# A hybrid trunk in fp32: gate and branch projections turned token-major, with 512 streamed weight columns

## Chip, cores and metric

The kernel runs on 1 core of a Trainium2 chip. The metric is the device time of one launch in microseconds; 977.33 is the median of three runs of the kernel before.

## What is computed

Two layers of a residual block on 256 tokens x 1024 channels, all in fp32. The part that the change touches is the parallel branches and their gated sum:

```python
u = rms_norm(h, norm_mix_pre[l])
proj = u @ w_in[l]
q, k, v, xr, yr, pp, gt = jnp.split(proj, SPLITS, axis=-1)
attn_br = sliding_window_attention(q, k, v, attn_sinks[l]) @ w_attn_br[l]
xc = causal_depthwise_conv(xr, conv_w[l], conv_b[l])
hr = rg_lru(xc, ...)
rnn_br = (hr * jax.nn.gelu(yr)) @ w_rnn_br[l]
pool_br = multi_scale_pool(pp, w_pool_groups[l], pool_scale[l]) @ w_pool_br[l]
g = jax.nn.sigmoid(gt).reshape(b, s, N_BRANCHES, D_MODEL)
merged = g[:, :, 0] * attn_br + g[:, :, 1] * rnn_br + g[:, :, 2] * pool_br
mix = merged @ w_out[l]
h = h + rms_norm(mix, norm_mix_post[l])
m = rms_norm(h, norm_mlp_pre[l])
h = h + rms_norm(jnp.square(jax.nn.relu(m @ w_mlp_up[l])) @ w_mlp_down[l], norm_mlp_post[l])
```

Each of the three gates and of the three branch projections is a 1024 x 1024 matrix.

## The kernel before

**Numbers.** Every fp32 operand is split into a high part (rounded to the `fp32r` format that TensorE multiplies) and a low part, the rest. A product is three matmuls, high x high, high x low and low x high (`mm3`, lines 88 to 91; these three lines stand for nearly all matmuls of the profile). The split is one ScalarE copy and one VectorE subtraction (`split`, lines 79 to 86).

**Weights.** They come as a stream of 512 KB half units [128, 1024] in the order of use: a DMA to `raw` (4 buffers), the split into `wh` and `wl` (8 buffers each; lines 81 and 82), then use. `take(n)` hands over the next n half units, `ahead()` asks for the splits of the two after them (lines 127 to 157).

**Two forms of a product.** In `w_unit` (line 273) the weights stand still: each 128x128 block of them is loaded and the 256 tokens are streamed past, so a matmul has 256 columns and the result is feature-major [128 features, 256 tokens]. One unit takes two half units and makes 256 features in one PSUM bank, with 48 matmuls. In `s_hu` (line 286) the tokens stand still: a 128x128 block of the activations is loaded and 512 weight columns are streamed past it, so the result is token-major [128 tokens, 512 features]; a half unit takes 6 matmuls per token tile, 12 for both. The output projection and the MLP's `down` use `s_hu`; `up`, the gates and the branches use `w_unit`. q, k, v use the token-major form by passes (`by_pass`, line 296).

**Order of the branch part.** The string `ORDER` lists the units: pp, yr, xr are input projections of the pool and recurrent branches, pg the pool's group products, gp/ga/gr the gates and bp/ba/br the branch projections (p pool, a attention, r recurrent), each 1024-column matrix in four units of 256. Every unit ends with `tick()`, a counter; `later(d, f)` runs f d ticks on. In this way the attention's scores, transposes and value products (four groups, scores at ticks 2, 7, 12 and 17; groups 1 and 3 are the large ones, with 256 keys, 4 score banks and 4 banks `pT` of transposed probabilities) and the recurrent gates are mixed into the projections. The instruction order of each engine is then fixed by a list scheduler at build time; `residual`, `mix_norm` and the transposes of `mlp_in(0)` run at a higher priority.

**Gated sum.** `gate` (line 600) makes th = tanh(x/2) on ScalarE from the unit's bank (line 603). `project` (line 607) forms (th + 1) times the projection on VectorE (lines 613 and 615), adds it to `merged[j]` (line 616), and, after the last branch (r), splits half of `merged[j]` into `mh`, `ml` (lines 84 and 85, tiles mgh and mgl in the profile), which are feature-major already.

**Output projection** (lines 638 to 663): eight half units, i = 0 to 3 for the first 512 output columns, contraction chunks 0-1, 2-3, 4-5, 6-7, and 4 to 7 for the second 512 columns. Token tile 0 runs through all eight, then tile 1; the post-norm `residual(0)` works meanwhile, and the transposes of `mlp_in(0)` (line 213, reading the updated `h`) are mixed into tile 1.

All PSUM tiles come from one pool of 8 banks.

Of the kernel before, what the change touches and what calls it, by code (L numbers as in the profile page):

```python
# [12 lines left out]
AF = mybir.ActivationFunctionType  # L13
# [5 lines left out]
T = 256  # L19
# [15 lines left out]
FINE = (8, 8)  # L35
SQRT_2_PI = 0.7978845608028654

# order of the units between q, k, v and the output projection: pp/yr/xr projections, pg pool groups,
# g gates and b branch projections of the branches p (pool), a (attention), r (recurrent)
ORDER = (  # L40
    "pp0 gp0 pp1 gp1 pp2 gp2 pp3 gp3 yr0 yr1 pg0 pg1 yr2 yr3 bp0 bp1 bp2 bp3 "
    "xr0 ga0 xr1 ga1 xr2 ga2 xr3 ga3 ba0 ba1 ba2 ba3 gr0 gr1 br0 gr2 br1 gr3 br2 br3"
).split()

# columns of the parameter tile, per layer
PG_PRE, PG_MLP, PCONVW, PCONVB, PBA, PBI, PLAM, PSCALE, PSINK = 0, 8, 16, 48, 56, 64, 72, 80, 88
NPAR = 104

# [1 line left out]
def trunk(ctx, tc, x, wts, rgw, par, gpost, eye, ctab, out):  # L50
# [19 lines left out]
    def ttile(shape, dt=F32, nm="t"):  # L70
        return tmp.tile(shape, dt, tag="t", name=nm)
# [7 lines left out]
    def split(hi, lo, src, scale=None):  # L79
        if scale is None:  # L80
            A.activation(hi, src, AF.Copy)  # L81
            V.tensor_tensor(out=lo, in0=src, in1=hi.bitcast(F32), op=ALU.subtract)  # L82
        else:
            A.activation(hi, src, AF.Copy, scale=scale)
            V.scalar_tensor_tensor(out=lo, in0=src, scalar=scale, in1=hi.bitcast(F32),
                                   op0=ALU.mult, op1=ALU.subtract)
# [3 lines left out]
        PE.matmul(o, lh, rl, start=False, stop=False, **kw)  # L90
        PE.matmul(o, ll, rh, start=False, stop=stop, **kw)  # L91

# [1 line left out]
    h = const.tile([P, 2, D], F32, name="h")  # L94
    idt = const.tile([P, P], F32, name="idt")
    cst = const.tile([P, ctab.shape[1]], F32, name="cst")
# [19 lines left out]
    for i in range(WARM):  # L116
        PE.matmul(wps[:], warm[:, 0:P], warm[:], start=True, stop=True)

# [1 line left out]
    NHU = wts.shape[0]  # L120
    st = {"load": 0, "split": 0, "use": 0}
    raw_t, hu_t = {}, {}
# [27 lines left out]
    def take(n):  # L150
        split_to(st["use"] + n)
        r = [hu_t.pop(st["use"] + i) for i in range(n)]
        st["use"] += n
        return r
# [10 lines left out]
    def tick():  # L165
        clock["n"] += 1
        run = [f for n, f in due if n <= clock["n"]]
        due[:] = [(n, f) for n, f in due if n > clock["n"]]
        for f in run:
            f()  # L170
# [2 lines left out]
        while due:  # L173
            tick()

# [1 line left out]
    hb = const.tile([P, L, 16], F32, name="hb")  # L177
    kk = const.tile([P, L, 8], F32, name="kk")
    nk2 = const.tile([P, L, 8], F32, name="nk2")
# [24 lines left out]
        V.tensor_scalar(kk[:], q, 2.0, None, op0=ALU.mult)  # L204
        V.tensor_scalar(nk2[:], q, -4.0, None, op0=ALU.mult)

# [1 line left out]
    def to_features(tt, src, gain, hi, lo, between=None):  # L208
        """src (token-major halves) * gain -> feature-major high and low parts."""
        tsl = slice(tt * P, (tt + 1) * P)  # L210
        banks = [bank([P, 4, P]) for _ in range(2)]
        for c in range(8):
            PE.transpose(banks[c // 4][:, c % 4, :], src[c // 4][:, (c % 4) * P:(c % 4 + 1) * P], ident)  # L213
        for half in range(2):
            if half and between:
                between()
            cs = range(4 * half, 4 * half + 4)
            for c in cs:
                A.activation(hi[:, c, tsl], banks[half][:, c % 4, :], AF.Copy, scale=gain[:, c:c + 1])  # L219
            for c in cs:  # L220
                V.scalar_tensor_tensor(out=lo[:, c, tsl], in0=banks[half][:, c % 4, :], scalar=gain[:, c:c + 1],
                                       in1=hi[:, c, tsl].bitcast(F32), op0=ALU.mult, op1=ALU.subtract)
# [25 lines left out]

    @hp
    def residual(tt, banks, scale, gB):  # L250
        """h[tt] += gB * scale * banks / rms(scale * banks)"""
        yg = []
        ss = stile(2)
        for nh in range(2):
            square_sum(banks[nh][:], ss[:, nh:nh + 1], scale)
            t = ttile([P, 512], nm="yg")
            gs = gB[:, nh * 512:(nh + 1) * 512]
            if isinstance(scale, float):
                V.tensor_tensor(out=t[:], in0=banks[nh][:], in1=gs, op=ALU.mult)
            else:  # L260
                V.scalar_tensor_tensor(out=t[:], in0=banks[nh][:], scalar=scale, in1=gs, op0=ALU.mult, op1=ALU.mult)
            yg.append(t)
        rs = rsqrt(total(ss))
        for nh in range(2):
            sl = slice(nh * 512, (nh + 1) * 512)
            V.scalar_tensor_tensor(out=h[:, tt, sl], in0=yg[nh][:], scalar=rs, in1=h[:, tt, sl],  # L266
                                   op0=ALU.mult, op1=ALU.add)
# [3 lines left out]
                acts.tile([P, NC_, T], F32R, tag="lo", name=nm + "l"))  # L271

    def w_unit(hus, xh, xl):
        """[128, 2, 256] = two column chunks of W (8 contraction chunks in 2 half units), times x."""
        ps = bank([P, 2, T])
        for n in range(2):
            for i, (wh, wl) in enumerate(hus):
                a = wh.rearrange("p (k n) -> p k n", k=4)
                b = wl.rearrange("p (k n) -> p k n", k=4)
                for k in range(4):  # L280
                    c = 4 * i + k
                    mm3(ps[:, n, :], a[:, k, n * P:(n + 1) * P], b[:, k, n * P:(n + 1) * P],
                        xh[:, c, :], xl[:, c, :], c == 0, c == 7)
        return ps
# [8 lines left out]
                start and k == 0, stop and k == 1)  # L293

    def by_pass(o, xh, xl, wh, wl, tt, mid=None):
        """Token-major product over 8 chunks, one pass after the other: the low parts are needed last."""
        tsl = slice(tt * P, (tt + 1) * P)
        for n, (xx, ww) in enumerate(((xh, wh), (xl, wh), (xh, wl))):
            for c in range(8):
                PE.matmul(o, xx[:, c, tsl], ww[c], start=(n == 0 and c == 0), stop=(n == 2 and c == 7))  # L300
                if mid and n == 2 and c == MID:
                    mid()
# [26 lines left out]
    un.append(mix_norm(1))  # L329

    for l in range(L):
# [1 line left out]
        qT = {}  # L333
        vt = []
        kTs = []
# [137 lines left out]
            later(ATT[2] + ATT[1] * gi, tr_)  # L473
            later(ATT[3] + ATT[1] * gi, pv_)

# [1 line left out]
        pmh = pml = rnh = rnl = mh = ml = None  # L477
        pooled, merged, gel, tails, ths = {}, {}, {}, [], {}

# [116 lines left out]
            split(xch[:], xcl[:], xc[:])  # L596
            later(RGD, lambda j=j, rgs=(rgh, rgl), xs=(xc, xch, xcl): rnn_gates(j, rgs, xs))

        def gate(br, j):
            ps = w_unit(take(2), uh, ul)  # L600
            tick()
            th = ttile([P, 2, T], nm="th")
            A.activation(th[:], ps[:], AF.Tanh, scale=0.5)
            ths[br, j] = th
            ahead()

        def project(br, j):
            ps2 = w_unit(take(2), *pairs[br])
            tick()
            th = ths.pop((br, j))  # L610
            if j not in merged:
                merged[j] = ttile([P, 2, T], nm="mg")
                V.scalar_tensor_tensor(out=merged[j][:], in0=th[:], scalar=1.0, in1=ps2[:], op0=ALU.add, op1=ALU.mult)
            else:
                V.scalar_tensor_tensor(out=th[:], in0=th[:], scalar=1.0, in1=ps2[:], op0=ALU.add, op1=ALU.mult)
                V.tensor_tensor(out=merged[j][:], in0=merged[j][:], in1=th[:], op=ALU.add)
            if br == ORDER[-1][1]:
                split(mh[:, 2 * j:2 * j + 2, :], ml[:, 2 * j:2 * j + 2, :], merged[j][:], scale=0.5)
            ahead()

        for nm in ORDER:
# [12 lines left out]
            else:  # L634
                {"pp": unit_pp, "pg": unit_pg, "yr": unit_yr, "xr": unit_xr}[kind](j)

# [1 line left out]
        gB = gpool.tile([P, D], F32, tag="g", name="gB")  # L638
        nc.sync.dma_start(gB[:], gpost[l, 0])
        mix = [[bank([P, 512]) for _ in range(2)] for _ in range(2)]  # L640
# [14 lines left out]
            later(3 + tt, mean_sq)  # L655

        for tt in range(2):
            for i in range(8):
                if tt == 1 and i == 6:
                    mlp_in(0)  # L660
                s_hu(mix[tt][i // 4][:], hus[i], mh, ml, 2 * (i % 4), tt, i % 4 == 0, i % 4 == 3)
            residual(tt, mix[tt], 1.0, gB)
        ahead()

# [1 line left out]
        gB = gpool.tile([P, D], F32, tag="g", name="gB2")  # L666
        nc.sync.dma_start(gB[:], gpost[l, 1])
        yb = [[bank([P, 512]) for _ in range(2)] for _ in range(2)]
# [77 lines left out]


def _w_units(w):
    """[1024, n] -> half units [128, 4 k, 256]: two per 256 columns."""
    n = w.shape[1] // 256  # L750
    return w.reshape(2, 4, P, n, 256).transpose(3, 0, 2, 1, 4).reshape(2 * n, P, HU_COLS)


def _s_units(w):
    """[k, n] -> [n/512][k/256] half units [128, 2 k, 512]."""
    kh, n = w.shape[0] // 256, w.shape[1] // 512
    return w.reshape(kh, 2, P, n, 512).transpose(3, 0, 2, 1, 4).reshape(n, kh, P, HU_COLS)

# [23 lines left out]
def _layout(i):  # L782
    qc = np.concatenate([np.arange(hd * 64, hd * 64 + 64) for hd in _HEADS])
    units, rg, par, gp = [], [], [], []
    for l in range(L):
# [5 lines left out]
        for u in _s_units(q):  # L791
            units.append(u)
        by = {"pg": i["w_pool_groups"][l].reshape(2, 2, 2, P, 256).transpose(0, 3, 1, 2, 4).reshape(2, 1, P, HU_COLS)}
        for nm, m in (("pp", pp), ("yr", yr), ("xr", xr), ("gp", gpl), ("ga", ga), ("gr", gr), ("bp", i["w_pool_br"][l]),
                      ("ba", i["w_attn_br"][l][qc]), ("br", i["w_rnn_br"][l])):
            by[nm] = _w_units(m).reshape(4, 2, P, HU_COLS)
        for nm in ORDER:
            units.append(by[nm[0:2]][int(nm[2])])
        for u in _s_units(i["w_out"][l]):
# [42 lines left out]
```

## Time and profile before

| | us |
|---|---|
| three runs | 975.85, 977.33, 978.89 |
| median | 977.33 |
| profiled execution, first to last instruction (span) | 975.3 |
| TensorE busy (matmul) | 962.2 (99%) |
| VectorE busy | 649.4 (67%) |
| ScalarE busy | 602.7 (62%) |

The profiled execution is one more run; the page gives its span only, which is 0.55 us under the shortest of the timed runs and 2.0 under their median. Matmuls are pipelined: each lasts longer than the distance to the next, so that the busy time of TensorE says whether it ever rests, and the distance between starts says how fast it goes. 16 DMA engines move 178 GB/s on average.

### The profile page before, as it was taken

To read this page: it belongs to the slowest core of one execution; us is meant where nothing else is said; L and a number is where in the kernel's file an instruction comes from. 1 tells how busy PE (TensorE), PEld (TensorE's weight loads), DVE (VectorE), ACT (ScalarE), POOL (GpSimd) and SP (SyncE) were. 2 spreads that over 40 slices of the span, in tenths; PEclk is the share of its full clock that TensorE was granted. 3 is DMA by queue.
4 is the path that set the end of the run, shared out by engine and by line. 5 is a ranking of instruction groups with operands and counts; after the bars stand their busy time and mean duration, and the time that the engine had idled before them with its cause. 6 is when DMAs were issued, how large, how long until landed. Compare 5 with 4: busy or idle time off the path is not lost.

```text
span 975.3 us, 17196 instructions
## 1 busy us (share of the span) xinstructions
PE 962.2 (99%) x6836; PEld 892.7 (92%) x6836; DVE 649.4 (67%) x1101; ACT 602.7 (62%) x1001; POOL 2.5 (0%) x20
## 2 busy tenths in 40 slices
PE   8999999999999999999999999999999999999997
PEld 5899999999998999999889999999999899999995
DVE  6877786679767754545586768766896585544542
ACT  7754764789637655455566657567895475655551
POOL 0000000000000000000000000000000000000000
PEclk9999999999999999999999999999999999999999
DMA  8756446443764766565457536535357376566531
GB/s 274 243 178 206 130 154 204 152 142 130 239 193 153 227 194 187 191 189 180 130 182 253 169 110 194 183 111 195 103 191 258 109 247 206 175 196 192 177 127 43
DMA packets 48751, 173.41 MB, mean 178 GB/s; under 512 B 5408, under 2 KB 5792, under 8 KB 48672
## 3 DMA queue, kind: packets, MB, share of 16 engines
q1 hardware_dynamic: 48384, 172.16, 55.6%
q8 instruction: 53, 0.87, 0.4%
q14 instruction: 26, 0.21, 0.1%
q10 hardware_dynamic: 288, 0.17, 0.1%
HBM read 171.26 MB, written 1.05 MB: 177 GB/s over the span
## 4 chain that ended last, share of the span: by engine, by line
PE 92%; DVE 3%; ACT 2%; DMA 2%; issue 1%; SPq 0%; DVEq 0%; ACTq 0%
PE ps L89 27%; PE ps L90 27%; PE ps L91 27%; PE ps L300 7%; DMA raw<-wts 2%; PE ps L436 1%; PE ps L388 1%; DVE wl L82 1%; PE ps L425 1%; ACT wh L81 1%; PE ps L213 1%; DVE xc L590 0%; PE ps L368 0%; DVE h L266 0%; ACT uh L219 0%
## 5 line engine op out<-in xcount | busy, mean ns | idle before, releaser
L82 DVE TENSOR_TENSOR wl<-raw,wh 128x1024 fp32r<-128x1024 f32 (+1 forms) x348 | 385.8, 1124 | 198.5 <-ACT wh L81 187.7
L81 ACT ACTIVATE wh<-raw 128x1024 fp32r<-128x1024 f32 (+1 forms) x348 | 334.7, 985 | 231.2 <-PE ps L90 115.8
L89 PE MATMUL ps<-uh,wh 128*128 128x256 f32 x768 | 218.7, 285 | 0.1
L90 PE MATMUL ps<-ul,wh 128*128 128x256 f32 x768 | 217.2, 283 | 0.0
L91 PE MATMUL ps<-uh,wl 128*128 128x256 f32 x768 | 217.2, 283 | 0.0
L89 PEld LDWEIGHTS ps<-uh,wh 128*128 128x128 f32 x768 | 147.2, 192 | 3.6 <-PE ps L436 1.6
L90 PEld LDWEIGHTS ps<-ul,wh 128*128 128x128 f32 x768 | 147.3, 192 | 0.1
L91 PEld LDWEIGHTS ps<-uh,wl 128*128 128x128 f32 x768 | 147.3, 192 | 0.0
L89 PE MATMUL ps<-mh,wh 128*128 128x256 f32 x448 | 126.9, 283 | 0.0
L91 PE MATMUL ps<-mh,wl 128*128 128x256 f32 x448 | 126.8, 283 | 0.0
L90 PE MATMUL ps<-ml,wh 128*128 128x256 f32 x448 | 126.8, 283 | 0.0
L90 PE MATMUL ps<-wl,hid 128*128 128x512 f32 x256 | 99.9, 390 | 0.0
L89 PE MATMUL ps<-wh,hid 128*128 128x512 f32 x256 | 99.8, 390 | 0.0
L91 PE MATMUL ps<-wh,hid 128*128 128x512 f32 x256 | 99.6, 389 | 0.0
L89 PEld LDWEIGHTS ps<-mh,wh 128*128 128x128 f32 x448 | 86.0, 192 | 0.5
L90 PEld LDWEIGHTS ps<-ml,wh 128*128 128x128 f32 x448 | 86.0, 192 | 0.5
L91 PEld LDWEIGHTS ps<-mh,wl 128*128 128x128 f32 x448 | 86.0, 192 | 0.0
L91 PEld LDWEIGHTS ps<-wh,hid 128*128 128x128 f32 x256 | 48.1, 188 | 10.1
L89 PEld LDWEIGHTS ps<-wh,hid 128*128 128x128 f32 x256 | 48.1, 188 | 9.6
L90 PEld LDWEIGHTS ps<-wl,hid 128*128 128x128 f32 x256 | 48.1, 188 | 9.4
L407 ACT ACTIVATE pr<-ps,s 128x128 f32<-128x128 f32 (+1 forms) x64 | 25.9, 432 | 33.1 <-DVE s L398 23.2
L89 PE MATMUL ps<-pmh,wh 128*128 128x256 f32 x128 | 36.6, 286 | 0.0
(188 smaller groups left out, 1589.5 us busy)
## 6 DMA issues: line engine op xcount, KB each, us to landing
raw<-wts SPq DMA_DIRECT2D x316, 512.0 KB, 4.4
gB<-gpost SPq DMA_DIRECT2D x4, 512.0 KB, 4.6
rg<-rgw SPq DMA_DIRECT2D x8, 256.0 KB, 4.2
out<-h SPq DMA_DIRECT2D x4, 256.0 KB, 2.0
h<-x SPq DMA_DIRECT2D x2, 256.0 KB, 3.5
h<-x SPq DMA_DIRECT2D x1, 512.0 KB, 7.6
cst<-ctab SPq DMA_DIRECT2D x1, 168.0 KB, 4.8
prm<-par ACTq DMA_DIRECT2D x1, 104.0 KB, 3.9
```

The costliest lines, as they stand in the source:

```text
L81: A.activation(hi, src, AF.Copy)
L82: V.tensor_tensor(out=lo, in0=src, in1=hi.bitcast(F32), op=ALU.subtract)
L89: PE.matmul(o, lh, rh, start=start, stop=False, **kw)
L90: PE.matmul(o, lh, rl, start=False, stop=False, **kw)
L91: PE.matmul(o, ll, rh, start=False, stop=stop, **kw)
L213: PE.transpose(banks[c // 4][:, c % 4, :], src[c // 4][:, (c % 4) * P:(c % 4 + 1) * P], ident)
L300: PE.matmul(o, xx[:, c, tsl], ww[c], start=(n == 0 and c == 0), stop=(n == 2 and c == 7))
L388: PE.matmul(sc[hd // hp][:, hd % hp, :], qT[a, j // 2][rows, j % 2, blk * P:(blk + 1) * P], kTs[0][rows, a, 0:w], start=True, stop=True)
L407: A.activation(pr[:, j, :], sc[i][:, j, :], AF.Exp, bias=negm[:, hd:hd + 1], accum_out=sums[:, hd:hd + 1])
L425: PE.transpose(ps[:, g, :], g8["p"](4 * b + g)[:, kt * P:(kt + 1) * P], ident)
L436: PE.matmul(ps[b * 64:b * 64 + 64, :, :], vt[kt][:, 256 + kv * 64:256 + kv * 64 + 64], g8[b, kt][:], start=(kt == 0), stop=(kt == nk - 1))
```

## The change

The gates and the branch projections go from `w_unit` to a new `t_unit`, which uses `s_hu`: one unit takes four half units and makes 512 features of all 256 tokens, in two PSUM banks (one per token tile), with 48 matmuls of 512 columns. Each matrix has two units instead of four, and `t_unit` ticks twice, so that a tick still falls after every two half units. The gated sum is then token-major, four tiles [128 tokens, 512 features]; `to_merged` transposes one of them on TensorE in four 128x128 blocks and splits the result from PSUM. The first feature half is transposed one tick after its last projection, inside the last unit; the second half is transposed within the output projection, whose half units run in the order 0, 1, 4, 5, 2, 3, 6, 7. The host lays out these six matrices as the output projection's. Lines of the changed kernel are 3 higher up to `unit_xr`.

```diff
+ORDER = (
+    "pp0 gp0 pp1 pp2 gp1 pp3 yr0 yr1 pg0 pg1 yr2 yr3 bp0 bp1 "
+    "xr0 ga0 xr1 xr2 ga1 xr3 ba0 ba1 gr0 gr1 br0 br1"
+).split()
+
+OUT_ORDER = (0, 1, 4, 5, 2, 3, 6, 7)
...
-        def gate(br, j):
-            ps = w_unit(take(2), uh, ul)
+        def t_unit(xh, xl, nh):
+            ps = [bank([P, 512]) for _ in range(2)]
+            for i in range(4):
+                hu, = take(1)
+                for tt in range(2):
+                    s_hu(ps[tt][:], hu, xh, xl, 2 * i, tt, i == 0, i == 3)
+                if i == 1:
+                    tick()
+                if i < 3:
+                    ahead()
             tick()
-            th = ttile([P, 2, T], nm="th")
-            A.activation(th[:], ps[:], AF.Tanh, scale=0.5)
-            ths[br, j] = th
+            return ps
+
+        def to_merged(nh, tt):
+            ps = bank([P, 4, P])
+            for i in range(4):
+                PE.transpose(ps[:, i, :], merged[nh, tt][:, i * P:(i + 1) * P], ident)
+            cs, tsl = slice(4 * nh, 4 * nh + 4), slice(tt * P, (tt + 1) * P)
+            split(mh[:, cs, tsl], ml[:, cs, tsl], ps[:], scale=0.5)
+
+        def gate(br, nh):
+            for tt, ps in enumerate(t_unit(uh, ul, nh)):
+                th = ttile([P, 512], nm="th")
+                A.activation(th[:], ps[:], AF.Tanh, scale=0.5)
+                ths[br, nh, tt] = th
             ahead()
 
-        def project(br, j):
-            ps2 = w_unit(take(2), *pairs[br])
-            tick()
...
+        def project(br, nh):
+            for tt, ps in enumerate(t_unit(*pairs[br], nh)):
+                th = ths.pop((br, nh, tt))
+                if (nh, tt) not in merged:
+                    merged[nh, tt] = m = ttile([P, 512], nm="mg")
+                    V.scalar_tensor_tensor(out=m[:], in0=th[:], scalar=1.0, in1=ps[:], op0=ALU.add, op1=ALU.mult)
+                else:
+                    m = merged[nh, tt]
+                    V.scalar_tensor_tensor(out=th[:], in0=th[:], scalar=1.0, in1=ps[:], op0=ALU.add, op1=ALU.mult)
+                    V.tensor_tensor(out=m[:], in0=m[:], in1=th[:], op=ALU.add)
+                if br == ORDER[-1][1] and nh == 0:
+                    later(1, lambda tt=tt: to_merged(0, tt))
             ahead()
...
         for tt in range(2):
-            for i in range(8):
-                if tt == 1 and i == 6:
+            for n, i in enumerate(OUT_ORDER):
+                if tt == 0 and n in (2, 5):
+                    to_merged(1, n // 5)
+                if tt == 1 and n == 6:
                     mlp_in(0)
```

What the scheduler makes of it is shown at three places; the order of instructions has no times. First TensorE of layer 0 from the last branch projection into token tile 1 of the output projection, before (wh_3527 to wh_3553 are the output projection's half units 0 to 4; the last rows lie in tile 1):

```order
L91 MATMUL ps<-rnh,wl_3467 128x256
L89 MATMUL ps<-wh_3527,mgh 128x512
...
L89 MATMUL ps<-wh_3553,mgh 128x512
L213 MATMUL ps<-idt,h 128x128 x8
L90 MATMUL ps<-wl_3554,mgh 128x512
```

And TensorE there in the changed kernel (wh_2941, 2963, 2983, 2989 and 2975 are the half units 0, 1, 4, 5 and 2 of the output projection, L619 is `to_merged`, L216 the transposes of `mlp_in`):

```order
L94 MATMUL ps<-wh_2871,rnl 128x512
L619 MATMUL ps<-idt,mg 128x128 x8
L92 MATMUL ps<-wh_2891,rnh 128x512
...
L92 MATMUL ps<-wh_2941,mgh 128x512
...
L94 MATMUL ps<-wh_2963,mgl 128x512
L619 MATMUL ps<-idt,mg 128x128 x4
L92 MATMUL ps<-wh_2983,mgh 128x512
...
L94 MATMUL ps<-wh_2975,mgl 128x512
L619 MATMUL ps<-idt,mg 128x128 x4
...
L216 MATMUL ps<-idt,h 128x128 x4
L92 MATMUL ps<-wh_2989,mgh 128x512
L216 MATMUL ps<-idt,h 128x128 x4
```

The eight transposes of the first feature half stand in the middle of br1, the other eight after 12 and after 30 matmuls of the projection; the transposes of `mlp_in(0)` stand 21 matmuls into tile 1, in two groups, where they stood 25 in.

Second, VectorE at the same place, before: the last two units' gated sums among the weight splits (L82).

```order
L615 SCALAR_TENSOR_TENSOR th<-th,ps 128x512
L82 TENSOR_TENSOR wl_3560<-raw_3557,wh_3559 128x1024
L616 TENSOR_TENSOR mg<-mg,th 128x512
L85 SCALAR_TENSOR_TENSOR mgl<-mg,mgh 128x512
L82 TENSOR_TENSOR wl_3566<-raw_3563,wh_3565 128x1024
```

VectorE there in the changed kernel, from the split of the first feature half on (L638 and L639 are `project`'s multiply and add, for the two token tiles of br1; L85 splits weights, L88 the merged sum):

```order
L88 SCALAR_TENSOR_TENSOR mgl<-ps,mgh 128x4x128 x2
L85 TENSOR_TENSOR wl_2996<-raw_2993,wh_2995 128x1024
L638 SCALAR_TENSOR_TENSOR th<-th,ps 128x512 x2
L639 TENSOR_TENSOR mg<-mg,th 128x512 x2
L85 TENSOR_TENSOR wl_3002<-raw_2999,wh_3001 128x1024
L88 SCALAR_TENSOR_TENSOR mgl<-ps,mgh 128x4x128 x2
```

Both multiplies stand together, then both adds, with no weight split between; one weight split stands ahead of the split of the second feature half.

Third, ScalarE after the first large score group (group 1 of layer 0), before: the exponentials, the copy of the pool unit ahead of it, and, six weight splits and a pool split later, the tanh of gp3.

```order
L407 ACTIVATE pr,s<-ps,s 128x256 x8
L410 ACTIVATE s<-s 128x8
L486 ACTIVATE xp<-ps 128x2x256
L81 ACTIVATE wh_1454<-raw_1319 128x1024
...
L81 ACTIVATE ph<-pd 128x512
L81 ACTIVATE wh_1683<-raw_1565 128x1024
L603 ACTIVATE th<-ps 128x512
```

In the changed kernel (L410 exponentials, L626 the tanh of gp1's two token tiles, L489 the copy of pp3):

```order
L410 ACTIVATE pr,s<-ps,s 128x256 x8
L413 ACTIVATE s<-s 128x8
L626 ACTIVATE th<-ps 128x512 x2
L489 ACTIVATE xp<-ps 128x2x256
L84 ACTIVATE wh_1358<-raw_1223 128x1024
```

The gate unit now stands ahead of the score group, and its two tanh follow the exponentials at once.

## Rows read from the trace of the kernel before

**Rows 1.** The page: busy time by engine, granted clock, chain of waits.

```profile
PE 962.2 (99%) x6836; PEld 892.7 (92%) x6836; DVE 649.4 (67%) x1101; ACT 602.7 (62%) x1001; POOL 2.5 (0%) x20
PEclk9999999999999999999999999999999999999999
PE 92%; DVE 3%; ACT 2%; DMA 2%; issue 1%; SPq 0%; DVEq 0%; ACTq 0%
```

**Rows 2.** Windows, layer 0: us, busy PE, PEld, DVE, ACT, POOL, PEclk, DMA, GB/s.

```profile
46.70:284.50 237.80, 237.67 (x1969) 231.25 (x1968) 181.50 (x328) 157.68 (x272) 0.88 (x6) 1.00 0.54 172
```

**Rows 3.** Waits of PE and its weight loader: us, times, longest.

```profile
PE ps L213 <- DVE h L266: 0.9, 1, 0.9
...
PEld ps L89 <- ACT mgh L84: 0.4, 2, 0.2
...
PEld ps L90 <- DVE wl L82: 0.4, 1, 0.4
```

**Rows 4.** Timeline of PE in the MLP: start us, duration us, instruction.

```profile
343.94 0.28 PE L89 MATMUL ps<-mh,wh 128*128 128x256 f32 x1
...
355.46 0.40 PE L89 MATMUL ps<-wh,hid 128*128 128x512 f32 x1
...
366.36 0.28 PE L89 MATMUL ps<-mh,wh 128*128 128x256 f32 x1
```

**Rows 5.** Window of PE, xr3 to the projection: us, busy, PEclk, DMA, GB/s.

```profile
199.60:284.50 84.90, 84.90 (x710) 1.00 0.56 179
```

**Rows 6.** Timeline of PE: 24 wide matmuls after transposes; 16 transposes.

```profile
41.11 0.48 PE L300 MATMUL ps<-wh,uh 128*128 128x512 f32 x1
...
46.68 0.28 PE L89 MATMUL ps<-uh,wh 128*128 128x256 f32 x1
...
110.39 1.91 PE L425 MATMUL ps<-idt,pr 128*128 128x128 f32 x16
112.06 0.37 PE L89 MATMUL ps<-ph,wh 128*128 128x256 f32 x1
```

**Rows 7.** Timeline after the scores of group 1, all engines.

```profile
91.24 0.60 ACT L81 ACTIVATE ath<-ps 128x512 fp32r<-128x512 f32 x1
92.36 0.68 DVE L82 TENSOR_TENSOR atl<-ps,ath 128x512 fp32r<-128x512 f32 x1
93.02 0.38 PE L89 MATMUL ps<-uh,wh 128*128 128x256 f32 x1
100.43 0.25 ACT L410 ACTIVATE s<-s 128x8 f32<-128x8 f32 x1
112.82 0.58 ACT L603 ACTIVATE th<-ps 128x512 f32<-128x512 f32 x1
```

**Rows 8.** Timeline at the hand-over to the output projection, DVE and ACT.

```profile
286.05 1.22 DVE L82 TENSOR_TENSOR wl<-raw,wh 128x1024 fp32r<-128x1024 f32 x1
287.19 0.69 DVE L616 TENSOR_TENSOR mg<-mg,th 128x512 f32<-128x512 f32 x1
287.91 0.63 ACT L84 ACTIVATE mgh<-mg 128x512 fp32r<-128x512 f32 x1 [2.19 <-DVE mg L616]
288.57 0.69 DVE L85 SCALAR_TENSOR_TENSOR mgl<-mg,mgh 128x512 fp32r<-128x512 f32 x1 [0.70 <-ACT mgh L84]
```

**Rows 9.** Timeline of PE and DVE: token tile 1 of the projection, post-norm.

```profile
295.56 0.39 PE L89 MATMUL ps<-wh,mgh 128*128 128x512 f32 x1
299.64 1.42 DVE L266 SCALAR_TENSOR_TENSOR h<-yg,s,h 128x512 f32<-128x512 f32 x2
301.23 1.04 PE L213 MATMUL ps<-idt,h 128*128 128x128 f32 x8
```

**Rows 10.** Timeline of PE and ACT after the recurrent gates of xr0.

```profile
191.10 2.04 ACT L427 ACTIVATE pT<-ps 128x512 f32<-128x512 f32 x4
191.33 0.28 PE L91 MATMUL ps<-xch,rgl 128*128 128x256 f32 x1
191.74 0.39 PE L89 MATMUL ps<-uh,wh 128*128 128x256 f32 x1
```

More of the change, by code (lines that the diff above doesn't have):

```diff
@@ L40 @@
 ORDER = (
-    "pp0 gp0 pp1 gp1 pp2 gp2 pp3 gp3 yr0 yr1 pg0 pg1 yr2 yr3 bp0 bp1 bp2 bp3 "
-    "xr0 ga0 xr1 ga1 xr2 ga2 xr3 ga3 ba0 ba1 ba2 ba3 gr0 gr1 br0 gr2 br1 gr3 br2 br3"
+    "pp0 gp0 pp1 pp2 gp1 pp3 yr0 yr1 pg0 pg1 yr2 yr3 bp0 bp1 "
+    "xr0 ga0 xr1 xr2 ga1 xr3 ba0 ba1 gr0 gr1 br0 br1"
 ).split()
+OUT_ORDER = (0, 1, 4, 5, 2, 3, 6, 7)
 PG_PRE, PG_MLP, PCONVW, PCONVB, PBA, PBI, PLAM, PSCALE, PSINK = 0, 8, 16, 48, 56, 64, 72, 80, 88
@@ L597, in unit_xr @@
             later(RGD, lambda j=j, rgs=(rgh, rgl), xs=(xc, xch, xcl): rnn_gates(j, rgs, xs))
-        def gate(br, j):
-            ps = w_unit(take(2), uh, ul)
-            tick()
-            th = ttile([P, 2, T], nm="th")
-            A.activation(th[:], ps[:], AF.Tanh, scale=0.5)
-            ths[br, j] = th
-            ahead()
-        def project(br, j):
-            ps2 = w_unit(take(2), *pairs[br])
-            tick()
[L610 to L618, printed above, removed]
+        def t_unit(xh, xl, nh):
[8 more added lines that the diff above has]
+                    ahead()
+            tick()
+            return ps
@@ L793, in _layout @@
         by = {"pg": i["w_pool_groups"][l].reshape(2, 2, 2, P, 256).transpose(0, 3, 1, 2, 4).reshape(2, 1, P, HU_COLS)}
-        for nm, m in (("pp", pp), ("yr", yr), ("xr", xr), ("gp", gpl), ("ga", ga), ("gr", gr), ("bp", i["w_pool_br"][l]),
-                      ("ba", i["w_attn_br"][l][qc]), ("br", i["w_rnn_br"][l])):
+        for nm, m in (("pp", pp), ("yr", yr), ("xr", xr)):
             by[nm] = _w_units(m).reshape(4, 2, P, HU_COLS)
+        for nm, m in (("gp", gpl), ("ga", ga), ("gr", gr), ("bp", i["w_pool_br"][l]), ("ba", i["w_attn_br"][l][qc]),
+                      ("br", i["w_rnn_br"][l])):
+            by[nm] = _s_units(m)
         for nm in ORDER:
```

## The prediction, made before the changed kernel ran

> **What bounds the kernel now.** I begin with the page's busy lines, its clock line and the chain of waits [rows 1]: TensorE is busy for 962.2 of 975.3 us, the granted clock is full in all 40 slices, and 92% of the chain that ended last is PE. VectorE stands at 67%, ScalarE at 62%. Next I look at the changed stretch alone [rows 2]: in layer 0's 237.8 us (layer 1's is like it) PE hardly rests, at clock 1.00, while DVE works 181.5 us and ACT 157.7. The waits table [rows 3] shows what is left to win by better feeding: PE waited 0.9 us for the residual, its weight loader twice 0.2 us for the split gated sum (mgh) and once 0.4 us for a weight split (L82). So the time is the number of PE instructions times their pace. Busy time does not give the pace: a 256-column matmul lasts 0.28 us and a 512-column one 0.39, but they overlap. The pace is the distance between starts, which the timeline gives.
>
> **Pace.** In the MLP both kinds stand side by side [rows 4]. From 343.94 to 355.46, 96 narrow matmuls (two half-stages of `up`, 48 each) take 11.52 us: 0.1200 each. From 355.46 to 366.36, 48 wide ones (`down`, which calls `s_hu` with two token tiles in turn, as the change will) take 10.90: 0.2271 each. In the branch stretch itself the last 84.9 us of layer 0 hold 14 units of 48 and three groups of 12 for the recurrent gates, 708 narrow ones: again 0.120 [rows 5]. At 2.4 GHz 256 columns are 106.7 ns and 512 are 213.3, so both kinds pay some 13.5 ns on top, whatever their width.
>
> **The change, part by part.**
> Matmuls: 6 matrices x 2 layers x 192 = 2304 narrow ones go, 1152 wide ones come, with the same columns in all. 2304 x 0.1200 = 276.5; 1152 x 0.2271 = 261.6; **-14.9 us**, all on the path.
>
> Here a rule speaks against it. The Trainium skill, "TensorE: Matmul & The Clock Gate", section "Back-to-back issue gap", gives a warm gap of N/2.4 + 2.5 ns. An estimate from it: 109.2 and 215.8 ns, so this term would be only 2304 x 109.2 - 1152 x 215.8 = 3 us and the change would come out about 1 us slower. The measured gaps are 120.0 and 227.1 ns, so the trace does not agree, and the measurement decides.
>
> Transposes: 32 new ones (16 per layer, 8 + 4 + 4). Sixteen of attention's take 110.39 to 112.06, 0.104 us each [rows 6]: **+3.3**. Each of the three groups per layer also cuts a stream: after transposes 24 wide matmuls take 41.11 to 46.68, 5.57 us, where 24 x 0.2271 is 5.45 [rows 6]. Six cuts at 0.12: **+0.7**.
>
> Evictions: per layer twelve tanh, twelve multiplies, eight adds and the four pairs of the merged split stay, with the same 128x512 elements. The split now reads PSUM; the split of the attention output from PSUM (L81, L82) stands beside it at 0.60 and 0.68 us against 0.63 and 0.69 from SBUF [rows 7, 8], so no time is added. The stretch gets 2% shorter, which takes DVE from 76% to 78%: not a bound. Weight bytes, DMAs and their number on SP stay; a half unit is used every 12 x 0.2271 = 2.73 us instead of 2.88. The cover is the head start of the splits, which the 0.4 us of the loader [rows 3] says is almost never used up. Counted at nothing; if it ran out, the next late thing would be a wl split of 1.22 us [rows 8].
>
> Hand-over to the output projection: before, the last gated sum ended at 287.88 and its split at 289.26, 4.8 us after br3's last matmul (284.4) [rows 8], and the loader paid its 0.2 us per layer [rows 3]. Now the order covers it: the first four chunks are transposed inside br1, the projection starts with half units 0, 1 (12 matmuls, 2.7 us), then 4 transposes, then 4 and 5 (2.7 us) before chunk 4 is wanted. DVE's order after br1 is two multiplies, then the adds: at 0.69 each [rows 8] 2.1 us to the first half, under 2.7. After the transposes come ACT's 0.63, one wl split of 1.22 that may stand ahead, and 0.69: 2.5 us, under 2.7. I take 0. If one more split stands ahead at either place, PE waits about 1 us: upper bound 2 places x 2 layers x 1.0 = 4 us; below, today's 0.2 per layer falls away (-0.4).
>
> Post-norm: mlp_in(0)'s transposes stood 25 matmuls into token tile 1, now 21. Tile 1 starts at 295.56, so they would stand at 300.33; h is written from 299.64 for 1.42 us, to 301.06 [rows 9]. First half about 300.4, second 301.06 with one matmul between: 0.2 us of waiting per layer, **+0.4**. From nothing to 1.1 (as if PE stood until 301.4) in each layer.
>
> Sum: -14.9 + 3.3 + 0.7 + 0.4 = -10.5 us. The profiled span 975.3 becomes 964.8. The three runs have their median at 977.33, 2.0 above that span; I keep this distance: 977.3 - 10.5 = **966.8 us**. About 0.3%, 2.9 us, is what a measurement here can tell from no change.
>
> **The rivals.**
> (a) Part of the gain is paid back in waits at the moved places: hand-over 4 us, post-norm 1.8 more, and wide matmuls that keep the pace after a cut (5.57/24 = 0.2321) rather than 0.2271, 1152 x 0.005 = 5.8. About half of these 11.6 gives 972.5. For it: DVE's queue mixes 1.2 us splits with everything. Against: `down` holds 0.2271 with the same calls.
> (b) The fixed 13.5 ns is not paid per matmul in the changed stage (it might hang on which operand stands still, weights before, tokens now). Then the first term vanishes but the transposes, cuts and waits stay: +4.4, 981.7; with a quarter of the term left, 978. The rule of the Trainium skill quoted above would end in the same place, near 979 by its own figures. Against this rival: the 708 matmuls of this very stage show it, and `down` keeps tokens still and has it once per 512 columns.
> (c) Slower: PSUM. All 8 banks are one pool. A gate unit now holds two until ACT's tanh, not one. In front of a large score group the tanh comes late: PE left the scores at 93.02, the exps end only at 100.7, and the tanh of the gate unit that PE ran from 93.02 to 98.8 (48 x 0.12) came at 112.82 [rows 7]. That the pool can bind is seen already: at 191.33 PE stood 0.3 us more than its pace, and went on at 191.74 as the first pT copy, begun at 191.10, was finishing [rows 10]. With two banks held for such 14 us beside 4 scores or 4 pT, PE would wait at two places: from 98.8 to 101.9 for the exps and two tanh, 3.1 us, and again for the fourth bank of pT, wanted at 110.39 + 12 x 0.104 = 111.6 and free at 112.82 + 0.58 = 113.4, 1.8 us: 5 us in each of 4 large groups (two per layer), +20, so 986.8. It decides from 2.6 us per group on. Against it: the changed order puts both tanh right behind the exps, and counting banks there (2 gate, 4 scores, 1 for the values, 1 next) gives exactly 8.
> (d) That it doesn't do what it says: the order on PE shows 128x512 matmuls in these places, so no.
>
> **How the numbers follow.** Forecast 0.75; (a) 0.16; (b) 0.05; (c) 0.04; (d) 0. Faster by over 0.3% means under 974.4: the forecast and three quarters of (a), 0.87. Within 0.3%: the far end of (a), 0.04, and the part of (b) with some gain left, 0.03, together 0.07. Slower: (c) and the rest of (b), 0.06. The low end is 966.8 less the post-norm wait (0.4), the hand-over at its lower bound (0.4), cuts that cost nothing (0.7), the 1.5 by which the lowest run lies under the median, and some 0.3 for reading the pace (0.01 us over 48 matmuls, times 1152): 963.5. The high end, 974.5, takes in two thirds of (a)'s 11.6 us; what lies above is the far end of (a), (b) and (c), 0.13, and little is left out below.
>
> **What would show it.** In the changed profile TensorE should have some 1120 matmuls fewer (1152 go, 32 come), starts 0.227 us apart in gates and branches, and each layer's stretch from pp0 to the output projection near 231 us (237.8 - 7.45 + 0.8 + 0.1); three groups of transposes of 0.4 to 0.8 us around the projection with next to no idle time before them; weight splits still never what PE waits for. I am wrong if the wide pace there is over 0.235, if PE idles before the new transposes or behind the score groups, or if its wait for the residual grows past 1 us per layer.

## The result, and the profile after

The changed kernel takes 964.6 us (median of four runs, 964.06 to 966.05) where the kernel before took 977.0 beside it (four runs, 975.85 to 978.89): a ratio of 0.9875, with an interval of 0.9861 to 0.9889. The profiled span is 962.3 us, 13.0 under the 975.3 of before.

The page of the changed kernel, the lines that answer to [rows 1]:

```profile
PE 951.3 (99%) x5716; PEld 835.3 (87%) x5716; DVE 649.7 (68%) x1101; ACT 599.8 (62%) x1001; POOL 2.6 (0%) x20
PEclk9999999999999999999999999999999999999999
PE 97%; DMA 1%; ACT 1%; DVE 1%; issue 0%; SPq 0%; DVEq 0%; ACTq 0%
```

TensorE issues 6836 - 5716 = 1120 matmuls fewer (1152 go, 32 transposes come), and it is still what everything hangs on: its share of the chain rises from 92 to 97%. DVE and ACT do the same 1101 and 1001 instructions in nearly the same time (649.7 us for 649.4, 599.8 for 602.7). The granted clock is full throughout, so nothing of the difference is a matter of the clock.

The windows of the two branch stretches, from the first matmul of pp0 to the last of br1, layer 0 and then layer 1 (columns as in [rows 2]):

```profile
46.30:277.30 231.00, 231.00 (x1401) 201.49 (x1400) 180.76 (x326) 155.68 (x271) 0.95 (x6) 1.00 0.54 178
518.80:749.90 231.10, 231.10 (x1401) 201.55 (x1400) 180.75 (x326) 156.91 (x272) 0.95 (x6) 1.00 0.55 178
```

Against [rows 2], 568 instructions of TensorE fewer and 6.8 us less; the weight loader, which had been busy for 97% of the stretch, now is for 87%, and DVE and ACT have the same work within 2 us. All stages side by side, each from the start of its first matmul to that of the next stage's:

| stage, us | before, layer 0 / 1 | after, layer 0 / 1 | difference |
|---|---|---|---|
| start, to the first branch stretch | 45.47 | 45.03 | -0.44 |
| branch stretch | 237.85 / 237.45 | 231.12 / 231.17 | -6.73 / -6.28 |
| output projection | 22.81 / 22.86 | 23.73 / 23.81 | +0.92 / +0.95 |
| first `up` stage of the MLP | 9.10 / 9.28 | 8.76 / 8.72 | -0.34 / -0.56 |
| rest of the MLP | 173.79 / 172.67 | 173.77 / 172.67 | -0.02 / 0.00 |
| layer 0 to layer 1 | 35.67 | 35.15 | -0.52 |
| end | 7.16 | 7.14 | -0.02 |

The branch stretches give 13.0, the projection takes 1.9, and stages in which no line was changed give another 1.9, a good half of it in the first `up` stages.

The timeline of TensorE in layer 0, from gr0 to the first `up` stage (columns: start us, duration us, instruction):

```profile
232.93 0.39 PE L92 MATMUL ps<-wh,uh 128*128 128x512 f32 x1
...
271.04 1.04 PE L619 MATMUL ps<-idt,mg 128*128 128x128 f32 x8
271.83 0.48 PE L92 MATMUL ps<-wh,rnh 128*128 128x512 f32 x1
...
280.09 0.60 PE L619 MATMUL ps<-idt,mg 128*128 128x128 f32 x4
280.44 0.47 PE L92 MATMUL ps<-wh,mgh 128*128 128x512 f32 x1
...
283.27 0.39 PE L92 MATMUL ps<-wh,mgh 128*128 128x512 f32 x1
...
284.63 0.60 PE L619 MATMUL ps<-idt,mg 128*128 128x128 f32 x4
284.99 0.47 PE L92 MATMUL ps<-wh,mgh 128*128 128x512 f32 x1
...
301.10 1.11 PE L303 MATMUL ps<-wh,mh 128*128 128x256 f32 x8
```

Three readings. From 232.93 to 271.04 there are 168 wide matmuls in 38.11 us: 0.2268 each, the pace of `down` in [rows 4]. The new transposes take 0.79 (eight), 0.35 and 0.35 us, 1.49 per layer, and none has an idle time before it. And a cut costs little: the 12 matmuls from 280.44 to 283.27 take 2.83 us, where 12 x 0.2268 is 2.72, so 0.11.

The timeline of VectorE at the hand-over (compare [rows 8]):

```profile
277.08 1.28 DVE L638 SCALAR_TENSOR_TENSOR th<-th,ps 128x512 f32<-128x512 f32 x2
278.27 1.28 DVE L639 TENSOR_TENSOR mg<-mg,th 128x512 f32<-128x512 f32 x2
...
281.35 0.69 DVE L88 SCALAR_TENSOR_TENSOR mgl<-ps,mgh 128x512 fp32r<-128x512 f32 x1 [0.66 <-ACT mgh L87]
```

The projection starts at 277.36. The gated sum is done at 279.55, 0.54 before its transposes start; its low half is split at 282.04, and the first matmul on these chunks starts at 283.27. Both places are covered, with about 0.5 and 1.2 us to spare. In the table of waits, PE and then its loader:

```profile
PE ps L216 <- DVE h L269: 0.2, 1, 0.2
...
PEld ps L93 <- DVE wl L85: 0.4, 1, 0.4
```

The 0.9 us for the residual became 0.2, the 0.4 for the gated sum is gone, the 0.4 for a weight split stays [rows 3]. Both waits for the residual stand before the transposes of the *second* token tile, in the first `up` stage of layer 1.

### The profile page after: what moved, and what is told of

The parts are those of the page before. It is cut to its first block, busy times and chain, and to the rows that moved or that the text cites. A ratio compares the mean times of both kernels' runs of the same rounds, so it can differ in the third digit from the quotient of the medians.

```text
span 962.3 us, 14953 instructions
## 1 busy us (share of the span) xinstructions
PE 951.3 (99%) x5716; PEld 835.3 (87%) x5716; DVE 649.7 (68%) x1101; ACT 599.8 (62%) x1001; POOL 2.6 (0%) x20
## 4 chain that ended last, share of the span: by engine, by line
PE 97%; DMA 1%; ACT 1%; DVE 1%; issue 0%; SPq 0%; DVEq 0%; ACTq 0%
PE ps L92 28%; PE ps L93 28%; PE ps L94 28%; PE ps L303 8%; PE ps L391 1%; PE ps L439 1%; PE ps L428 1%; DMA raw<-wts 1%; PE ps L216 1%; PE ps L371 0%; PE ps L619 0%; ACT wh L84 0%; DVE h L269 0%; ACT junk L229 0%; DVE wl L85 0%
## 5 line engine op out<-in xcount | busy, mean ns | idle before, releaser
L85 DVE TENSOR_TENSOR wl<-raw,wh 128x1024 fp32r<-128x1024 f32 (+1 forms) x348 | 385.7, 1123 | 189.1 <-ACT wh L84 180.4
L92 PE MATMUL ps<-uh,wh 128*128 128x256 f32 x384 | 109.0, 284 | 0.0
L93 PE MATMUL ps<-ul,wh 128*128 128x256 f32 x384 | 108.7, 283 | 0.0
L94 PE MATMUL ps<-uh,wl 128*128 128x256 f32 x384 | 108.6, 283 | 0.0
L92 PE MATMUL ps<-wh,uh 128*128 128x512 f32 x200 | 79.2, 396 | 0.7 <-ACT uh L222 0.7
L94 PE MATMUL ps<-wh,ul 128*128 128x512 f32 x200 | 78.1, 390 | 0.4 <-DVE ul L224 0.4
L93 PE MATMUL ps<-wl,uh 128*128 128x512 f32 x200 | 78.1, 390 | 0.0
L92 PEld LDWEIGHTS ps<-uh,wh 128*128 128x128 f32 x384 | 73.6, 192 | 1.1 <-issue 0.7
L93 PEld LDWEIGHTS ps<-ul,wh 128*128 128x128 f32 x384 | 73.6, 192 | 0.4
L94 PEld LDWEIGHTS ps<-uh,wl 128*128 128x128 f32 x384 | 73.6, 192 | 0.0
```

Source lines behind the costliest of these rows:

```text
L92: PE.matmul(o, lh, rh, start=start, stop=False, **kw)
```

## The experiments

Where the expectations name a theory by a letter, each says what it stands for; the prediction's own is that the width of the matmuls sets the gain, with transposes and cuts to be paid. Ratios are to the kernel before, run beside each.

**1. Narrow matmuls in the new form.** Everything of the change stays, tokens standing still included, but each 512-column matmul of gates and branches is issued as two of 256.

```diff
+            for s in range(0, 512, w):
+                mm3(ps[:, s:s + w], xh[:, c0 + k, tsl], xl[:, c0 + k, tsl], a[:, k, s:s + w], b[:, k, s:s + w],
+                    start and k == 0 and s == 0, stop and k == 1 and s + w == 512)
...
-                    s_hu(ps[tt][:], hu, xh, xl, 2 * i, tt, i == 0, i == 3)
+                    s_hu(ps[tt][:], hu, xh, xl, 2 * i, tt, i == 0, i == 3, 256)
```

> The changed kernel, but in the gate and branch units each 512-column matmul is issued as two of 256 columns (same tokens standing still, same banks). Theory A (a matmul pays some 13.5 ns on top of its columns, whatever stands still): 1152 matmuls more at 2 x 0.1200 instead of 0.2271, so +14.9 us on 964.6: 979.5, and starts 0.120 us apart in those units. Theory B (the gain comes from tokens standing still instead of weights, not from the width): no change, 964.6. In between, 972, would mean both.

Measured: 978.75 us (978.01 to 979.19), ratio 1.0022 [1.0013, 1.0031]. The timeline of TensorE in the same stretch, gr0 to the first transposes:

```profile
238.22 0.28 PE L92 MATMUL ps<-wh,uh 128*128 128x256 f32 x1
...
278.52 1.03 PE L620 MATMUL ps<-idt,mg 128*128 128x128 f32 x8
```

336 matmuls in 40.30 us, 0.1199 each, as `w_unit`'s had been with the weights standing still [rows 5]. The stretch takes 2.19 us more than with 168 wide ones, 13.0 ns for each matmul saved. The branch stretches are 238.31 and 238.35 us, 7.19 and 7.18 over the changed kernel's, and the whole kernel 14.15. So the gain comes from the width, and none of it from which operand stands still; the new form with narrow matmuls is even slower than before, since it pays for the transposes. Width here means the number of matmuls and with it that of weight loads, one for each: in this stretch the loader is busy for all of the 40.30 us, and in the changed kernel for 31.48 of the 38.11.

**2. Four times as narrow.** The same with 128 columns, to see whether a fixed cost per matmul explains it at every width.

```diff
-                    s_hu(ps[tt][:], hu, xh, xl, 2 * i, tt, i == 0, i == 3)
+                    s_hu(ps[tt][:], hu, xh, xl, 2 * i, tt, i == 0, i == 3, 128)
```

> The changed kernel with each 512-column matmul of the gate and branch units issued as four of 128 columns: 4608 matmuls in place of 1152. If the 13.5 ns on top stay the same at any width: 53.3 + 13.5 = 66.8 ns each, 4608 x 0.0668 - 261.6 = +46, 1011. If a matmul cannot go faster than its weight load, with the 0.104 to 0.109 us at which 128-column transposes go one after another: 4608 x 0.107 - 261.6 = +231, 1196.

Measured once: 1217.18 us. The same stretch on TensorE:

```profile
317.23 0.22 PE L92 MATMUL ps<-wh,uh 128*128 128x128 f32 x1
...
392.21 0.62 PE L620 MATMUL ps<-idt,mg 128*128 128x128 f32 x4
```

672 matmuls in 74.98 us: 0.1116 each. A fixed 13.5 ns on top of 128 columns (53.3 ns at 2.4 GHz) would be 0.067. So it is not one cost that holds at all widths: between 256 and 128 columns the distance hardly falls any more. The expectation's second sum, by the pace of transposes, came nearer (1196). The loader is busy for all of the 74.98 us; whether it is the weight load that goes with every matmul, or something else, was not separated. What the row settles is that a matmul of 128 columns takes almost as long as one of 256.

**3. Without the transposes.** `to_merged` splits the token-major tile as it lies; the transposition is left out of the computation, and everything else is issued as before.

```diff
-            ps = bank([P, 4, P])
-            for i in range(4):
-                PE.transpose(ps[:, i, :], merged[nh, tt][:, i * P:(i + 1) * P], ident)
...
-            split(mh[:, cs, tsl], ml[:, cs, tsl], ps[:], scale=0.5)
+            split(mh[:, cs, tsl], ml[:, cs, tsl], merged[nh, tt][:].rearrange("p (c n) -> p c n", c=4), scale=0.5)
```

> The changed kernel without its 32 transposes: the gated sum is split as it stands, token-major, into the place of the feature-major one; the transposition is left out, so the output projection multiplies other numbers. Theory A (the transposes cost what they last, 3.0 us, and cuts of the stream 0.7, with the waits around them covered): 964.6 - 3.7 = 960.9. Rival (the longer output projection only takes time that PE would otherwise wait for the residual behind it): 963 to 964.6, with the wait before the second token tile's transposes of mlp_in grown by what the projection lost.

Measured: 960.98 us (960.58 to 961.44), ratio 0.9841 [0.9828, 0.9854], 3.6 under the changed kernel. Each branch stretch (230.23, 230.27) and each projection (22.88, 22.87) is 0.9 us shorter, and the first `up` stage is the same (8.81, 8.73). So transposes and their cuts cost 3.6, at the two places where they stand. The wait for the residual is 0.5 us here, and `up` is no longer: a longer projection is not what hides the post-norm.

**4. The projection in its plain order**, so that the second feature half is wanted at once.

```diff
-OUT_ORDER = (0, 1, 4, 5, 2, 3, 6, 7)
+OUT_ORDER = (0, 1, 2, 3, 4, 5, 6, 7)
```

> The changed kernel with the output projection's half units in the order 0 to 7, so that chunk 4 is wanted almost at once after its transposes (the scheduler puts 4 matmuls of half unit 4 in between). Theory A (hand-over is covered by the order 0, 1, 4, 5): without it PE waits for ACT 0.63, a weight split that may stand ahead 1.22 and DVE 0.69, less 4 matmuls 0.9, so 0.5 to 1.9 us per layer: 965.5 to 968.5. Rival (it was never on the path): 964.6 within 0.5.

Measured: 966.47 us (965.97 to 967.17), ratio 0.9899 [0.9884, 0.9915]. The number lies in the range, but not for its reason: the projections are unchanged (23.69, 23.71), and the loss stands in the first `up` stages, 9.15 and 10.20. The waits of PE, then of its loader:

```profile
PE ps L216 <- DVE h L269: 2.2, 2, 1.6
...
PEld ps L92 <- ACT mgh L87: 0.4, 2, 0.2
...
PEld ps L94 <- DVE mgl L88: 0.4, 2, 0.2
```

The hand-over without its cover costs the loader 0.8 us, and the projection is no longer by it; what grew is the wait for the second token tile's residual in the post-norm. A weight transfer that leaves later is behind it; the part on the prediction has the rows.

**5. That order alone, in the kernel before.** If it were the order that shortened the first `up` stage, it should do so here.

```diff
-            for i in range(8):
-                if tt == 1 and i == 6:
+            for n, i in enumerate((0, 1, 4, 5, 2, 3, 6, 7)):
+                if tt == 1 and n == 6:
```

> The kernel before with nothing but the output projection's order 0, 1, 4, 5, 2, 3, 6, 7. The changed kernel won 1.9 us outside the branch stretch and the projection, 0.9 of it in the wait for the residual before the MLP. Theory C (the new order of the half units frees buffers or the post-norm earlier): 977.0 - 1 to 2 = 975 to 976, with the wait before mlp_in's transposes of token tile 1 down from 0.9 to 1.2 us to about 0.4. Theory D (the projection is 0.9 us longer while the weight DMA that holds up ScalarE is not, so its lateness is covered): no change, 977.0 within 0.6.

Measured: 976.62 us (eleven runs, 974.99 to 978.89) against 976.52 (twenty-one), ratio 1.0002 [0.9993, 1.0011]. So the times show no gain from the order by itself: the interval allows 0.7 us less to 1.1 more. The profiled execution, the slowest of the eleven, doesn't settle the question of the first `up` stage: it takes 9.97 us in layer 0 and 8.87 in layer 1, where the kernel before has 9.10 and 9.28. In the same profile TensorE waited 1.0 us for a copy of pT in layer 0, where the profile of the kernel before has 0.13.

**6 and 7. One PSUM bank less,** in the changed kernel and in the kernel before. The prediction had counted all eight banks as needed by the changed one.

```diff
-    psum = ctx.enter_context(tc.tile_pool(name="psum", bufs=8, space=PSUM))
+    psum = ctx.enter_context(tc.tile_pool(name="psum", bufs=7, space=PSUM))
```

> The changed kernel with 7 PSUM banks in the pool instead of 8. My bank count at the large score groups was exactly 8 (2 gate, 4 scores, 1 values, 1 next), so with 7 PE should wait there: until the exps and two tanh are done in each of four large groups, up to 3 us each: 964.6 + 4 to 12 = 968 to 977, idle time of PE behind the score groups. Rival (banks are nowhere near binding): 964.6 within 1.

> The kernel before with 7 PSUM banks. If the changed kernel's two banks per unit bring it nearer to the limit than the kernel before, this loses less than the changed kernel does with 7: 977.0 + 0 to 4, in the place after xr0's recurrent gates (0.3 us with 8). Rival (both lose the same, since the scheduler orders around the pool): the same loss as the changed kernel's.

Measured: the changed kernel 964.8 us (964.29 to 966.09), ratio 0.9876 [0.9858, 0.9894], nothing lost; the kernel before 980.16 (nine runs, 979.68 to 981.43) against 976.9, ratio 1.0034 [1.0023, 1.0044], 3.3 us lost. My count was wrong, and it was the kernel before that stood near the limit. Its waits with seven banks:

```profile
PE ps L89 <- ACT th L603: 2.3, 2, 1.1
...
PE ps L89 <- ACT pT L427: 1.2, 2, 0.6
```

They are the two waits that rival (c) had priced for the changed kernel, the late tanh [rows 7] and the copy of pT [rows 10], once per layer each. In the changed kernel the tanh runs from 99.0 us right behind the exponentials, and neither wait appears with eight or with seven banks.

**8. Wide matmuls in the first `up` stage as well.** It is token-major already, in passes of 256 columns; here its weights come as half units of the projection's layout and its passes have 512.

```diff
...
-                for u in range(2):
-                    w = [[t_.rearrange("p (k n) -> p k n", k=4)[:, k, :] for hu in hus[2 * u:2 * u + 2]
-                          for k in range(4) for t_ in hu[i:i + 1]] for i in range(2)]
-                    by_pass(ps[:, u * 256:(u + 1) * 256], uh, ul, w[0], w[1], tt,
-                            mid=(lambda: mlp_in(1)) if tt == 0 and u == 1 else None)
+                by_pass(ps[:], uh, ul, w[0], w[1], tt, mid=(lambda: mlp_in(1)) if tt == 0 else None)
...
-        units.append(up[0])
+        units.append(_s_units(i["w_mlp_up"][l])[0])
```

> The changed kernel with the MLP's first up unit (token-major already, by passes, in 256-column halves) in 512 columns: 96 narrow matmuls per layer become 48 wide. Theory A: 2 x 0.62 = 1.2 us less, 963.4, if the weights are there; all four half units are wanted in the first pass instead of two, so up to 2 us per layer of waiting for weight splits could take that back: 963.4 to 967.

Measured: 962.76 us (962.43 to 963.13), ratio 0.9851 [0.9835, 0.9866], 1.8 under the changed kernel and the fastest here that computes the whole. 96 narrow matmuls become 48 wide ones in each layer (5716 - 5620 = 96 fewer in all); at 13 ns for each that goes, that is 96 x 0.013 = 1.2 us. Between the two profiles the MLP, from its first `up` stage on, is shorter by 0.5 us in layer 0 and 0.6 in layer 1; where the rest of the 1.8 comes from is not shown.

**9. The other seven `up` units token-major too.** Each then needs eight transposes of its own. (The cuts leave out the definition of `hidden_T` and a `tick` among the last `down` half units.)

```diff
-            for u in range(2):
-                ps = w_unit(take(2), uh, ul)
+            ps = [bank([P, 512]) for _ in range(2)]
+            for i in range(4):
+                hu, = take(1)
+                for tt in range(2):
+                    s_hu(ps[tt][:], hu, uh, ul, 2 * i, tt, i == 0, i == 3)
...
+            later(1, lambda: hidden_T(0))
+            later(1, lambda: hidden_T(1))
```

> The changed kernel with the other seven up units of each MLP token-major too: 96 narrow matmuls become 48 wide (-0.62 us) and the hidden tile is then transposed (8 transposes at 0.099, +0.79, and a cut, +0.12 or more). Here every unit needs a transposition of its own, where six gate and branch matrices share one. Theory A: 14 x (+0.3) = +4, 968.6 to 970. Rival (token-major is worth it whatever follows): under 964.

Measured: 967.61 us (967.29 to 967.68), ratio 0.9902 [0.9886, 0.9919], 3.0 over the changed kernel. TensorE from one `up` to the next `down`:

```profile
336.39 0.39 PE L92 MATMUL ps<-wh,mh 128*128 128x512 f32 x1
...
341.84 1.03 PE L746 MATMUL ps<-idt,z 128*128 128x128 f32 x8
342.63 0.48 PE L92 MATMUL ps<-wh,mh 128*128 128x512 f32 x1
...
348.16 0.39 PE L92 MATMUL ps<-wh,hid 128*128 128x512 f32 x1
```

48 wide matmuls and eight transposes take 11.77 us. The same stage of the changed kernel, 96 narrow ones:

```profile
337.34 0.28 PE L92 MATMUL ps<-mh,wh 128*128 128x256 f32 x1
...
348.86 0.40 PE L92 MATMUL ps<-wh,hid 128*128 128x512 f32 x1
```

It takes 11.52. The width wins 96 x 0.1199 - 48 x 0.2271 = 0.6 and the transposes cost 0.79 and a cut: 0.25 us lost, fourteen times, 3.5. In the branch part twelve such units (six matrices) share two such transpositions; here each pays for its own.

## Why the prediction was right, point by point

**The matmul term**, -14.9, is the cause, and nearly the right size: undoing the width alone costs 14.4 in the branch stretches (7.19 + 7.18) and 14.15 in the whole time. The pace behind it, 0.120 and 0.227 us, is found again in the changed stretch (0.1199 narrow in experiment 1, 0.2268 wide). The prediction's sentence that the fixed share is paid "whatever their width" is true of the two widths in the sum only: at 128 columns the share is 58 ns (experiment 2).

**Rival (b)**, that the pace hangs on what stands still, falls with experiment 1: same operand still, half the width, and the gain is gone. The Trainium skill, "TensorE: Matmul & The Clock Gate", section "Back-to-back issue gap", gives a gap of N/2.4 + 2.5 ns, which it calls that of an isolated matmul; for a stream it says that the formula gives too little at small N and too much at large N. The prediction had set it against a stream without saying so, and had an estimate near 979 from it. By the formula two narrow matmuls cost 2.6 ns more than a wide one. The runs show 2 x 119.9 - 226.8 = 13.0 ns and 964.6 us: they do not agree, at 512 columns the stream lies above the formula's 215.8 and not below, and the measurement decides.

**Transposes and cuts**, +3.3 and +0.7, measured together 3.6 by experiment 3. The transposes alone take 2 x 1.49 = 3.0, a little less than the 0.104 us each that attention's rows gave, which leaves 0.6 for the cuts.

Branch stretch and projection by themselves came out as forecast: 13.0 less in the two stretches, where the sum says -14.9 with half of the transposes (1.66) and two of the cuts (0.24), so -13.0; 1.9 more in the projections, where 16 transposes and four cuts make 2.1.

**Evictions and weights, 0:** right. DVE's and ACT's busy times stand, and the loader's one wait of 0.4 us is the same.

**Hand-over, 0:** right. 2.1 and 2.5 us of work had been set against 2.7 of cover; the rows show the sum ready 0.54 us and its split 1.2 us ahead of need. But the cover mattered less than I thought: without it (experiment 4) the projection is no longer, and what the order does change is the first `up` stage.

**Post-norm, +0.4: this is the term that failed**, in its place and in its sign. I had put 0.2 us per layer on the transposes of the first token tile, which stand inside the projection; no idle time is recorded before them, in either kernel. The 0.9 us of [rows 3] stands before those of the second tile, in the first `up` stage of layer 1:

```profile
791.44 0.41 PE L213 MATMUL ps<-idt,h 128*128 128x128 f32 x2 [0.88 <-DVE h L266]
```

At the same place in layer 0 the kernel before idles another 0.65 us. The changed kernel idles 0.06 and 0.17 there, and the first `up` stages, which I held fixed, are 0.9 us shorter together. Where it comes from is seen ahead of that stage on VectorE, SyncE and ScalarE, after, and below it before:

```profile
294.54 1.89 DVE L85 TENSOR_TENSOR wl<-raw,wh 128x512 fp32r<-128x512 f32 x3
296.46 0.33 SPq L134 DMA_DIRECT2D raw<-wts  x1
300.97 1.16 ACT L84 ACTIVATE wh<-raw 128x512 fp32r<-128x512 f32 x2 [0.66 <-DMA raw<-wts]
302.03 0.58 ACT L229 ACTIVATE junk<-ps 128x512 f32<-128x512 f32 x1
```

```profile
300.97 1.29 DVE L82 TENSOR_TENSOR wl<-raw,wh 128x512 fp32r<-128x512 f32 x2
302.17 0.68 DVE L259 TENSOR_TENSOR yg<-ps,gB 128x512 f32<-128x512 f32 x1
302.77 1.28 DVE L82 TENSOR_TENSOR wl<-raw,wh 128x512 fp32r<-128x512 f32 x2
303.55 0.33 SPq L131 DMA_DIRECT2D raw<-wts  x1
307.81 1.15 ACT L81 ACTIVATE wh<-raw 128x512 fp32r<-128x512 f32 x2 [1.07 <-DMA raw<-wts]
308.86 0.58 ACT L226 ACTIVATE junk<-ps 128x512 f32<-128x512 f32 x1
```

The second square of the second tile's post-norm (L229, before L226) stands behind a weight split that waits for its DMA. The stage's first matmul starts at 301.10 after and 307.34 before, so the square comes 0.93 us into it now and came 1.52 in before. In experiment 4 the split waits 1.11 us in layer 0 and 2.17 in layer 1, where the changed kernel's waits 0.66 and 0.72, and the stages are the longer for it. So the stage follows the landing of one weight transfer, which the prediction had not looked at.

That transfer leaves as soon as VectorE's third weight split after the first tile's residual has ended, which gives its buffer back: 0.02 to 0.4 us later in both layers of all eleven profiles. In the plain order the first 512 columns of token tile 1 are complete after four half units, and the post-norm's multiply (`yg`, L259) gets in front of that third split; in the order 0, 1, 4, 5, 2, 3 they are complete after six, and the three splits stand together. In the three kernels with the plain order (the one before, with eight and with seven banks, and experiment 4) the transfer leaves 3.55 to 3.87 us ahead of the stage, in the eight with the new order, experiment 5 among them, 4.64 to 4.73. So it is the order of the half units that lets it leave earlier. From there to its landing it takes 3.88 to 6.00 us. The 6.00 stands in layer 0 of experiment 5, whose first `up` stage lasts 9.97 us; in its layer 1 the transfer takes 4.59 and the stage 8.87. How much of the 0.9 us is the order's stays open, since experiment 5's times show no gain; over the nine kernels with this stage unchanged it takes 8.46 to 10.20 us.

**The rest of what the forecast missed.** Forecast -10.5, measured -12.4 between the medians and -13.0 between the two profiled spans. The range held it with 1.1 us to spare, but by allowances made for other things (the hand-over, the cuts, the scatter of the runs): it had none for a shorter `up` stage, and that is luck. The difference in the spans, 2.5, is the 0.4 of the post-norm, 0.2 in the projections and the 1.9 in stages without a changed line: 0.9 in `up`, 0.44 at the start, 0.52 between the layers. At the start no instruction differs, and that stage takes 44.30 to 45.80 us over the kernels run, so I count it as scatter. Between the layers the kernel before takes 35.16 us too when it has seven banks, so a shift of waits elsewhere is enough for that half microsecond; which one, was not pursued.

**Rival (c)**, the banks: its mechanism is real and its place was wrong. It strikes the kernel before with one bank less, at 3.3 us and not 20. In the changed kernel both tanh stand right behind the exponentials, and neither wait appears; that it is this order that keeps it out was not tested by itself. **Rival (a)**: no new wait took anything back.

## What to carry to other kernels

When TensorE never rests and its clock is full, its time is the number of matmuls times the distance between their starts: read that distance off two rows with a known count between them, for each width, and look for the same work with fewer, wider matmuls. Which operand stands still is then a choice of width alone, and its price is the transposition of the result, so it pays where several matrices add into one result that is transposed once (0.6 us won per 1024 x 512 unit against 0.8 to 0.9 per transposition), or where the result is token-major already (experiment 8). Before a count of banks is made a rival, ask how long each kernel holds them: here the one whose gate units hold a single bank was nearer to the limit than the one whose units hold two. And a transfer that a change doesn't touch can still leave earlier or later by it: look for what gives its buffer back.

## What was not expected of the hardware

The distance between starts is 0.1116 us at 128 columns, 0.1199 at 256 and 0.2268 at 512, in the same stretch at the full clock: it all but stops falling below 256, so that at 128 streamed columns a column costs nearly twice what it costs at 512. And the first `up` stage, whose matmuls are the same in nine of the kernels, took 8.46 to 10.20 us; in the changed kernel, the one before and experiment 4, ScalarE's queue stood there 0.66 to 2.17 us for a single weight transfer, with the post-norm's square behind it, and that transfer took from 3.88 to 6.00 us over all the profiles.
